# Reordering one layer's late work: raw weights fetched ahead of their casts, r loaded with the decay, bonus halves ahead of y's scaling, the turning copy of an inverse on the engine that makes it

## The chip, the cores and the metric

The kernel runs on one core of a Trainium2 chip. The metric is the device time of one execution in microseconds (us). The core has five engines with an instruction stream each: TensorE (PE, matrix products), VectorE (DVE), ScalarE (ACT), GpSimd (POOL) and SyncE (SP), which here issues every DMA. An engine runs its instructions strictly in the written order.

## The reference

One inference step of a trunk with two layers of width 1024. 1024 prompt tokens (with 16 meta tokens ahead) and 8 sequences of 8 sampled tokens go through it. Layer 0 is a gated DeltaNet, layer 1 an RWKV-7 mixer; a final RMSNorm follows.

```python
def rwkv_mixer(xn, S0, shift_prev, mu, w_rkvz, ...):
    xs = xn[None] + (xprev - xn)[None] * mu[:, None, None, :]         # token shift, mixed per projection
    r, k, v, z = einsum('sbtd,sde->sbte', xs[:4], w_rkvz)             # 1024 x 1024 each
    w = -softplus(-(w0 + tanh(xs[4] @ w1) @ w2)) - 0.5                # decay through a small rank
    a = sigmoid(a0 + (xs[5] @ a1) @ a2)
    kk = l2norm(k * k_k per head);  k = k * (1 + (a - 1) * k_a)
    decay = exp(-exp(w))
    # per head (16 heads of 64), token by token:
    #   S = S * decay - (S kk) (kk a)^T + v k^T ;  y = S r
    # then a GroupNorm per head, + sum(r * k * r_k) * v (the bonus), * silu(z), @ w_o, residual
```

In the kernel the recurrence is done in chunks of 64 tokens; each chunk needs the inverse of a triangular matrix.

## The kernel before, in words

Layer 0 fills the first 1190 us and the norm, the decay and the key projection of layer 1 go on to 1398; the change leaves them alone. What follows has two stages. In both, every engine's order is the order in which the code writes its instructions (a manual schedule); no planner moves anything.

**Projections (1398 to 1782 us).** `projections` writes 67 products of 24 matmuls for r, v and z (tile `d`, a ring of accumulators). After every 12 matmuls comes a gap, and `plan[g]` holds what other engines do in gap `g`, sorted by its last argument: casts and fetches of weight halves (`wraw` raw, `whi` and `wlo` the high and low half of an fp32 number in two narrower ones), the mixes of the token shift, the evacuations `out`. Beside it run the preparations of the recurrence. There are 24 items: 8 head pairs by 3 segments of 384, 384 and 336 tokens. `system_steps` makes each one's decayed keys and stores them (`ald`, `kpd`, `k2d`). Five items make a batch (the last has four). `system_inverse` turns a batch's 120 matrices of 32x32 into inverses (31 steps of two operations, L690 and L692, on GpSimd), ACT copies them transposed (L1647), and SP stores both forms (`r_t`, `r_u`). `system_diagonals` and `system_merge` read them back (`TL`, `sTT`), and `mZ` and `mU` on PE join the 32-blocks to 64-blocks, which go to memory as `ttd`.

**Recurrence (1782 to 2199 us).** `wave` runs 54 steps (`tau`), two per item, so that several items are under way. A step has the phases 0, 1, 1.5, 2 and 3; `put(tau, phase, f, prio)` in `rwkv_item` says where an item's parts are written, and lower `prio` comes first in a phase. Item n starts at T = 2n. Its parts: `load` (cs is the summed decay, r the receptance), `exps` (`fDp`), `reads` (`AR` = r times decay), `pair` (`pr`), `halves` (`prh` on ACT, `prl` on GpSimd), `scores` (`G`), `bonus` (`fbonus` on PE), `keys` (`BT`). `rwkv_finish` scales y with the GroupNorm's factor `grs` on GpSimd (L1953) and multiplies by the gate `lz`. `rTT` is the loaded inverse, `Sb` and `x` are rows of the final norm and the residual sum. `fill`, at prio 2.5 in phase 2 and 1 in phase 3, writes the work that isn't in the chain: what is left of z's product (`dz` and `zo` tiles), and the output projection. Their weights come from `Stream`: `fetch` issues the load of a raw half (L66), `cast` splits it (high on ACT, low on GpSimd), `take` hands one out and refills. Raw halves have two buffers. 58 halves come through it: 10 of z, then 16 for each of the three segments' output projection.

The functions, by line numbers of the profile:

Of the kernel before, what the change touches and what calls it, by code (L numbers as in the profile page):

```python
# [25 lines left out]
class Gaps:  # L26
# [3 lines left out]
    def put(self, g, f, prio=2):  # L30
        self.q.setdefault(max(g, self.now), []).append((prio, f))
# [23 lines left out]
class Stream:  # L55
# [13 lines left out]
    def cast(self):  # L69
        if self.made < len(self.srcs):  # L70
            hi, lo = (self.b.t(self.b.wp, [128, 4, 128], n, self.b.WB, F32R) for n in ("whi", "wlo"))
            self.b.split(self.raw.pop(self.made), hi, lo)
            m = self.srcs[self.made].shape[2]
            self.w[self.made] = [x.rearrange("p a b -> p (a b)").rearrange("p (k m) -> p k m", m=m) for x in (hi, lo)]
            self.made += 1

    def take(self):
        self.used += 1
        while self.made < min(len(self.srcs), self.used + 2):
            self.cast()  # L80
            self.fetch()
        return self.w.pop(self.used - 1)


# [4 lines left out]
class Builder:  # L89
# [581 lines left out]
        L.put(ends[2] + 8, store, 3)  # L671
        return out

    def inverse_open(self, nb, pool):

        T = self.t(pool, [128, 1024], "invT", 1)[0:nb]
        self.nc.gpsimd.memset(T, 0.0)
        self.nc.gpsimd.memset(T[:, 0:1024:33], 1.0)
        return T

    def inverse_steps(self, A, nb, pool, T=None, eng=None):

        nc = self.nc
        v = eng or nc.vector
        T = self.inverse_open(nb, pool) if T is None else T
        Tv = T.rearrange("p (i j) -> p i j", j=32)
        for j in range(31):
            n, m = 31 - j, j + 1
            tmp = self.t(pool, [128, 256], "invtmp", 1)[0:nb, 0:n * m].rearrange("p (n m) -> p n m", m=m)
            v.tensor_tensor(tmp, A[:, j, j + 1:32].unsqueeze(2).broadcast_to([nb, n, m]),  # L690
                            Tv[:, j, 0:m].unsqueeze(1).broadcast_to([nb, n, m]), op=ALU.mult)
            v.tensor_tensor(Tv[:, j + 1:32, 0:m], Tv[:, j + 1:32, 0:m], tmp, op=ALU.subtract)  # L692
            yield Tv
# [880 lines left out]
    def system_steps(self, Q, B):  # L1574

        nc, t, col, pool = self.nc, self.t, self.pcol, B.pool
        pc = lambda x: col[x][:, Q.p:Q.p + 1]
        q = Q.n - B.items[0]
        cs, a, k = (Q.ld[x] for x in ("cs", "a", "k"))
        c6 = lambda x: x.rearrange("p (c i) -> p c i", i=64)  # L1580
        kk, iD = t(pool, [128, 384], "skk", 3), cs
        al, sq = t(pool, [128, 384], "sal", 3), t(pool, [128, 384], "sqs", 3)
        self.act(al[:, 1:384], cs[:, 0:383], AF.Exp, scale=-self.DEC)
        nc.vector.memset(c6(al)[:, :, 0:1], 1.0)
        if Q.s == 0:
            nc.vector.memset(al[:, 0:64].rearrange("p (b r) -> p b r", r=8)[:, :, 0:1], 1.0)
        self.act(sq, k, AF.Square, scale=pc("rwkv_k_k"))
        nc.vector.scalar_tensor_tensor(kk, k, pc("rwkv_k_k"), a, op0=ALU.mult, op1=ALU.mult)
        nc.vector.scalar_tensor_tensor(al, k, pc("rwkv_k_k"), al, op0=ALU.mult, op1=ALU.mult)
        self.act(iD, cs, AF.Exp, scale=self.DEC)  # L1590
        nc.vector.tensor_tensor(kk, kk, iD, op=ALU.mult)
        yield
        self.act(a, a, AF.Identity, scale=pc("rwkv_k_a"), bias=self.omka[:, Q.p:Q.p + 1])
        yield
        ssp = self.ps("f", 2, "rss")
        for c in range(6):
            for h in (0, 1):
                b = slice(64 * h, 64 * h + 64)
                self.mm(ssp[b, c:c + 1], sq[b, 64 * c:64 * c + 64], self.ones[b, 0:1])
        gp = self.ps("f", 2, "L")  # L1600
        for c in range(6):
            for h in (0, 1):
                b, d = slice(64 * h, 64 * h + 64), slice(64 * c, 64 * c + 64)
                self.mm(gp[b, d], al[b, d], kk[b, d])
        nc.vector.tensor_tensor(a, a, k, op=ALU.mult)
        nc.vector.tensor_tensor(a, a, iD, op=ALU.mult)
        nc.sync.dma_start(self.ald[Q.n], al)
        yield
        rk = self.rk2[:, 6 * Q.n:6 * Q.n + 6]
        nc.vector.tensor_scalar(rk, ssp[:, 0:6], 1e-6, None, op0=ALU.add)  # L1610
        nc.vector.reciprocal(rk, rk)
        nc.sync.dma_start(self.kpd[Q.n], kk)
        nc.vector.tensor_tensor(c6(sq), c6(gp[:, 0:384]), rk.unsqueeze(2).broadcast_to([128, 6, 64]), op=ALU.mult)
        if Q.s == 0:
            nc.gpsimd.tensor_tensor(sq[:, 0:64], sq[:, 0:64], self.m_strs2, op=ALU.mult)
        nc.sync.dma_start(self.k2d[Q.n], a)
        yield
        yield
        yield
        nc.sync.dma_start(B.ltd[6 * q:6 * q + 6].rearrange("c q i -> q c i"), c6(sq))  # L1620
# [18 lines left out]
    def system_inverse(self, B):  # L1639

        nc, t, nth, pool = self.nc, self.t, B.nth, B.pool
        nb = 4 * nth
        Av = B.A.rearrange("p (i s) -> p i s", s=32)
        inv = self.inverse_steps(Av.rearrange("p i s -> p s i"), nb, pool, eng=nc.gpsimd)
        for Tv in inv:
            yield
        nc.scalar.copy(Av, Tv.rearrange("p i j -> p j i"))  # L1647
        yield
        ud = self.dram([nb, 1024], f"r{B.b}_u")
        t1d = self.dram([nb // 2, 1024], f"r{B.b}_t")  # L1650
        nc.sync.dma_start(t1d, Tv[0:nb // 2].rearrange("p i j -> p (i j)"))
        nc.sync.dma_start(ud, B.A)
        yield
        yield
        B.TL = t(pool, [128, 30, 32], "TL", 1)[:, 0:nth]
        tv = t1d.rearrange("(c p) (s i) -> p s c i", p=2, s=32)
        for p in (0, 1):
            nc.sync.dma_start(B.TL[64 * p + 32:64 * p + 64], B.ltd[:, 64 * p + 32:64 * p + 64, 0:32].rearrange("c i s -> i c s"))
            nc.sync.dma_start(B.TL[64 * p:64 * p + 32], tv[p])
        B.uv = ud.rearrange("(r c p) (s i) -> r p s c i", r=2, p=2, s=32)  # L1660
# [40 lines left out]
    def rwkv_item(self, n, put):  # L1701

        nc, t, col = self.nc, self.t, self.pcol
        P = Ctx()
        s, p = divmod(n, 8)
# [93 lines left out]
            put(T - 3, 0, lambda: nc.gpsimd.memset(self.UVs[n], 0.0), 4)  # L1799
        if 0 < n < 3:  # L1800
            put(T - 3, 0, lambda: nc.gpsimd.memset(self.TTz[n], 0.0), 4)
        put(*((T - 5, 1) if n else (-4, 0)), lambda: load("cs"), 0)
        put(T - 4, 0, lambda: load("r"), 0.1)
        put(T - 4, 1, lambda: load("k2", "al"), 0)
        put(T - 4, 2, lambda: load("v", "kp"), 0)
        put(*((T - 4, 2) if n else (-3, 1)), exps, 2)
        put(T - 4 if n else -3, 3 if n else 2, reads, 6 if n else -1.5)
        put(T - 1 - (n < 3), 2 + (n < 3), lambda: load("tt"), 0)
        put(T - 3, 2, pair, 1.5)
        put(T - 2, 2, halves, 2.3)  # L1810
        put(T - 2, 1, lambda: scores(0), 2)
        put(T - 2, 2, values, 2.05)
        put(T - 1, 2, bonus, -1)
        put(T - 1, 1, lambda: scores(3), 2)
        put(T - 1, 2, lambda: keys(0), 3)
        put(T - 1, 3, lambda: keys(3), 3)
        if s == 0:
            read = self.rwkv_sample_read(P)
            go = lambda: next(read, None)
# [585 lines left out]
    def projections(self, xa, xb, ip, opened, tiles, whi, wlo, fetch, cast):  # L2405
# [8 lines left out]
        def put(g, f, late=2):  # L2414
            plan[g].append((late, f))
# [63 lines left out]
        for B in batches:  # L2479
            g = g0(B.items[-1]) + 9  # L2480
            B.TT, B.m = {}, {}
            put(g, lambda B=B: self.system_diag(B))
            inv = self.system_inverse(B)
            g = at = max(at + 4, g + 2)
            for u in range(31):
                put(g + u // 2, lambda inv=inv: next(inv, None), 3)
            at += 16
            steps(at, inv, 4, 3)
            g = at + 4
            for q in range(len(B.items)):  # L2490
                put(g + 2 * q + (3 if q == 4 else 0), lambda B=B, q=q: self.system_diagonals(B, q))

                def begin(B=B, q=q):
                    B.m[q] = self.system_merge(B, q)
                    next(B.m[q])
                put(g + 4 + 2 * q, begin)
                for u in range(1, 7):
                    put(g + 4 + 2 * q + u, lambda B=B, q=q: next(B.m[q], None), 1)
# [9 lines left out]
        zin = tuple([f[:, x, k, 0:SEGS[2][1]] for k in range(8)] for x in (0, 1))  # L2508
        self.stream = Stream(self, self.late_weights())
        for u, f_ in ((-1, self.stream.fetch), (-1, self.stream.fetch), (2, self.stream.cast), (2, self.stream.fetch),  # L2510
                      (4, self.stream.cast), (4, self.stream.fetch)):
            put(g + u, f_, 0)

        put(118, opened, 0)
# [8 lines left out]
        for ti, s in order:  # L2523
            m, k = tiles[ti]
            dst = {0: self.rd, 2: self.vd, 3: self.zd}[m]
            for c0, n in SEGS[s:s + 1]:
# [3 lines left out]
                def out(p=p, c0=c0, n=n, m=m, k=k, dst=dst):  # L2530
# [3 lines left out]
                    else:  # L2534
                        nc.scalar.copy(f[:, 0:n], p[:, 0:n])
                    put(now[0] + 2, lambda: nc.sync.dma_start(dst[k][:, c0:c0 + n], f[:, 0:n]))
                put(now[0], out, 0)
        while now[0] < len(plan):
            gap()
        return zin  # L2540
# [1 line left out]
    def wave(self, zin, stay, last, pool):  # L2542
# [63 lines left out]
            put(14 + 16 * s, 3, lambda s=s: residual(s), 4)  # L2606
        for steps, s in more:
            for u, k in steps.items():
                put(*((int(u), 2, lambda s=s, k=k: norm(s, k), 2.55 if s else 2.45) if u == int(u) else (int(u), 3, lambda s=s, k=k: norm(s, k), 5)))

        at = lambda tau: [(P[n], tau - 2 * n) for n in range(max(0, (tau - 4) // 2), min(24, tau // 2 + 1)) if 0 <= tau - 2 * n < 6]
        emit(-4, 3)
# [70 lines left out]
```

## Time and profile before

| what | value |
|---|---|
| three runs | 2209.49, 2211.76, 2212.59 us; median 2211.76 |
| the profiled execution | 2200.45 us; span of its trace 2198.7 us |
| busy share of PE, DVE, ACT, POOL | 95%, 66%, 57%, 57% |
| mean granted clock of PE | 0.981 |
| matmuls | 20958 |
| bytes moved | 291.67 MB, mean 133 GB/s |

The shares are means over the whole span, of which the changed part is the last 800 us. A row of the windows view gives, for a stretch in us, its length and then the busy time of PE, its weight loads, DVE, ACT and POOL with their instruction counts, the clock that PE was granted (1.00 is full), the busy share of the 16 DMA engines, and GB/s. A row of the waits reads: the engine and line that waited, what it waited for, us in total, how often, the longest. A row of the timeline: start, duration, engine, line, operation, tiles, and in brackets the idle time ahead of it and what ended it. A group's row ends with busy us, mean ns of one, idle time before.

### The profile page before, as it was taken

How to read it: one execution, taken by the hardware profiler on the slowest of the kernel's cores; microseconds unless marked ns; L12 is line 12 of the kernel's file. 1: busy time of each engine (PE TensorE's matmuls, PEld its weight loads, DVE VectorE, ACT ScalarE, POOL GpSimd, SP SyncE). 2: the span in 40 equal slices, each digit the busy share in tenths (PEclk: the TensorE clock that was granted, in tenths of full speed). 3: DMA queues.
4: the chain of work that ended last, by engine and by line, in shares of the span. 5: the costliest groups of instructions: out<-in, count | busy, mean ns of one | idle time of the engine just before them, and what ended most of it. 6: DMA issues, size and time to landing. Idle time of an engine off the chain costs nothing.

```text
span 2198.7 us, 56155 instructions
## 1 busy us (share of the span) xinstructions
PE 2084.4 (95%) x20958; PEld 1943.7 (88%) x20958; DVE 1447.7 (66%) x3682; ACT 1261.0 (57%) x3627; POOL 1242.7 (57%) x1858
## 2 busy tenths in 40 slices
PE   8999999999999999989999999998999998899997
PEld 7888989898999989878999999998889986788886
DVE  7868585866757585975436762778656346777865
ACT  6536565656656564645533564755646465676763
POOL 3428677685858585625341451238568645676664
PEclk9999999999999999999999999999999999999998
DMA  4324242424243342426344235587785665665543
GB/s 122 87 71 122 74 126 73 118 72 114 80 118 97 86 124 69 134 72 181 98 136 124 69 107 180 181 253 200 219 250 148 166 181 146 174 170 165 162 129 109
DMA packets 510763, 291.67 MB, mean 133 GB/s; under 512 B 240777, under 2 KB 495866, under 8 KB 510490
## 3 DMA queue, kind: packets, MB, share of 16 engines
q1 hardware_dynamic: 510490, 288.08, 46.7%
q8 instruction: 166, 2.72, 0.5%
q14 instruction: 107, 0.88, 0.1%
HBM read 195.66 MB, written 92.30 MB: 131 GB/s over the span
## 4 chain that ended last, share of the span: by engine, by line
PE 51%; DVE 16%; POOL 9%; issue 8%; DMA 6%; ACT 6%; SPq 3%; DVEq 0%; POOLq 0%; ACTq 0%
PE d L129 13%; PE dz L129 7%; PE dv L129 6%; PE rA L129 5%; PE do L129 3%; DVE cvy L634 3%; POOL y L1953 2%; PE dk L129 2%; PE dq L129 1%; PE dlora L129 1%; PE zo L129 1%; DVE invtmp L690 1%; DVE invT L692 1%; DMA wraw<-in_gdn_w_out 1%; POOL wlo L143 1%
## 5 line engine op out<-in xcount | busy, mean ns | idle before, releaser
L143 POOL TENSOR_TENSOR wlo<-wraw,whi 128x512 fp32r<-128x512 f32 x190 | 255.3, 1344 | 219.7 <-ACT whi L139 204.7
L692 POOL TENSOR_TENSOR invT<-invT,invtmp 72x31 f32<-72x31 f32 (+36 forms) x341 | 213.9, 627 | 26.7
L634 DVE SCALAR_TENSOR_TENSOR cvy<-raw,cw,cvy 128x408 f32<-128x408 f32 (+2 forms) x288 | 203.3, 706 | 29.6 <-ACT cvy L115 25.4
L690 POOL TENSOR_TENSOR invtmp<-invA,invT 72x31 f32<-72x31 f32 (+36 forms) x341 | 203.6, 597 | 26.1 <-DMA invA<-rltd 5.6
L129 PE MATMUL d<-xc,whi 128*128 128x384 f32 (+1 forms) x640 | 177.1, 342 | 0.0
L139 ACT CAST whi<-wraw 128x512 fp32r<-128x512 f32 x238 | 146.0, 615 | 31.3 <-DMA wraw<-in_rwkv_w_o 12.4
L129 PE MATMUL dv<-xc,whi 128*128 128x384 f32 (+1 forms) x480 | 154.2, 342 | 0.0
L129 PE MATMUL dz<-xc,whi 128*128 128x384 f32 (+1 forms) x480 | 152.3, 340 | 0.0
L1953 POOL TENSOR_SCALAR y<-y,mv,grs 128x64 f32<-128x64 f32 x132 | 82.3, 643 | 90.8 <-DVE grs L164 90.8
L115 ACT ACTIVATE w<-rA,nbp 128x128 f32<-128x128 f32 x144 | 45.2, 364 | 153.4 <-PE rA L129 151.0
L129 PEld LDWEIGHTS d<-xc,whi 128*128 128x128 f32 x640 | 118.1, 192 | 2.0 <-ACT ev L1441 0.3
L129 PE MATMUL d<-xc,wlo 128*128 128x384 f32 (+1 forms) x320 | 105.0, 338 | 2.1 <-DVE wlo L143 2.1
L160 POOL TENSOR_TENSOR ors<-ovar,cvals 128x6 f32<-128x6 f32 x24 | 34.1, 1421 | 125.7 <-DVE ovar L1122 125.7
L129 PE MATMUL dz<-xa,whi 128*128 128x384 f32 (+1 forms) x288 | 102.8, 357 | 0.5 <-DVE zg L906 0.5
L129 PE MATMUL d<-xa,whi 128*128 128x384 f32 (+1 forms) x336 | 95.9, 338 | 7.2 <-ACT whi L139 6.0
L129 PE MATMUL dv<-xa,whi 128*128 128x384 f32 (+1 forms) x288 | 102.1, 354 | 0.0
L959 POOL TENSOR_SCALAR Sb<-Sb,eglb 128x128 f32<-128x128 f32 x128 | 88.9, 707 | 5.7 <-DVE usc L752 3.0
L129 PEld LDWEIGHTS dv<-xc,whi 128*128 128x128 f32 x480 | 88.9, 188 | 3.5 <-issue 3.0
L129 PEld LDWEIGHTS dz<-xc,whi 128*128 128x128 f32 x480 | 89.8, 190 | 0.6 <-issue 0.2
L129 PE MATMUL d<-xh,whi 128*128 128x384 f32 (+1 forms) x256 | 82.9, 336 | 0.9 <-ACT xh L139 0.9
L129 PE MATMUL d<-xl,whi 128*128 128x384 f32 (+1 forms) x256 | 83.0, 337 | 0.2 <-DVE xl L143 0.2
L129 PE MATMUL d<-xh,wlo 128*128 128x384 f32 (+1 forms) x256 | 82.5, 336 | 0.0
(557 smaller groups left out, 7288.7 us busy)
## 6 DMA issues: line engine op xcount, KB each, us to landing
wraw<-in_gdn_w_in SPq DMA_DIRECT2D x96, 256.0 KB
wraw<-in_rwkv_w_rkvz SPq DMA_DIRECT2D x74, 256.0 KB
Sb<-in_state_gdn SPq DMA_DIRECT2D x64, 256.0 KB
wraw<-in_rwkv_w_o SPq DMA_DIRECT2D x48, 256.0 KB
E<-drow SPq DMA_DIRECT2D x24, 384.0 KB
attn<-drow SPq DMA_DIRECT2D x24, 384.0 KB
wraw<-in_gdn_w_out SPq DMA_DIRECT2D x36, 256.0 KB
out_s_gdn<-Sb SPq DMA_DIRECT2D x32, 256.0 KB
```

The costliest lines, as they stand in the source:

```text
L115: return self.nc.scalar.activation(out, in_, func, bias=bias, scale=scale, **kw)
L129: self.nc.tensor.matmul(out, lhsT, rhs, start=start, stop=stop)
L139: nc.scalar.copy(hi, x)
L143: e.tensor_tensor(lo, x, hi.bitcast(F32), op=ALU.subtract)
L160: self.nc.gpsimd.tensor_tensor(y, x, half.broadcast_to(sh), op=ALU.pow)
L634: nc.vector.scalar_tensor_tensor(ys[s][:, 0:wd(s)], raws[s][:, k:k + wd(s)], cw[k], ys[s][:, 0:wd(s)], op0=ALU.mult, op1=ALU.add)
L690: v.tensor_tensor(tmp, A[:, j, j + 1:32].unsqueeze(2).broadcast_to([nb, n, m]), Tv[:, j, 0:m].unsqueeze(1).broadcast_to([nb, n, m]), op=AL ...
L692: v.tensor_tensor(Tv[:, j + 1:32, 0:m], Tv[:, j + 1:32, 0:m], tmp, op=ALU.subtract)
L959: nc.gpsimd.tensor_scalar(Sb[g][:, u], Sb[g][:, u], self.eglb[:, hv, 4 * g + u:4 * g + u + 1], None, op0=ALU.mult)
L1953: nc.gpsimd.tensor_scalar(y[:, q], y[:, q], mv[:, q, 0:1], P.rs[:, q:q + 1], op0=ALU.subtract, op1=ALU.mult)
```

## The change

- **Inverses.** The transposing copy moves from ACT to the engine that made the inverse. For batches 0 to 3 this is GpSimd; batch 4's whole inverse (62 operations and the copy) moves to VectorE, three columns per gap from gap 112. The gaps of the batches are now a written table: inverses from 27, 47, 67, 87 and 112, stores and what follows them from 46, 66, 86, 106 and 124. For batches 0 to 3 stores, loads, diagonals and merges are two gaps later than before (44, 64, 84, 104); batch 4's stay (124).
- **Stores and evacuations.** The stores of `ald` and `kpd` are written two gaps and one gap later, each evacuation of `d` one gap later.
- **Stream.** `take` fetches the next raw half and then casts the present one; before, it cast one and fetched the one after the next. One fetch at the start goes. The last 16 low halves are made on VectorE.
- **Loads.** r is loaded together with the decay, three phases earlier.
- **Bonus.** `halves` goes from prio 2.3 to -0.3 in its phase.
- **Others.** `keys(3)` goes ahead of `fill`; the first final norm's parts ahead of it too (2.45 to 0.45).

```diff
@@ Stream @@
-            self.b.split(self.raw.pop(self.made), hi, lo)
+            self.b.split(self.raw.pop(self.made), hi, lo, eng_lo="pool" if self.made < 42 else "dve")
...
         while self.made < min(len(self.srcs), self.used + 2):
+            self.fetch()
             self.cast()
-            self.fetch()
@@ system_steps @@
-        nc.sync.dma_start(self.ald[Q.n], al)
         yield
...
-        nc.sync.dma_start(self.kpd[Q.n], kk)
...
         nc.sync.dma_start(self.k2d[Q.n], a)
         yield
+        nc.sync.dma_start(self.ald[Q.n], al)
+        nc.sync.dma_start(self.kpd[Q.n], kk)
         yield
@@ system_inverse @@
-        inv = self.inverse_steps(Av.rearrange("p i s -> p s i"), nb, pool, eng=nc.gpsimd)
+        eng, tag = (nc.vector, "") if B.b == 4 else (nc.gpsimd, "")
+        inv = self.inverse_steps(Av.rearrange("p i s -> p s i"), nb, pool, eng=eng, tag=tag)
         for Tv in inv:
             yield
-        nc.scalar.copy(Av, Tv.rearrange("p i j -> p j i"))
+        eng.tensor_copy(Av, Tv.rearrange("p i j -> p j i"))
@@ rwkv_item @@
-        put(*((T - 5, 1) if n else (-4, 0)), lambda: load("cs"), 0)
-        put(T - 4, 0, lambda: load("r"), 0.1)
+        put(*((T - 5, 1) if n else (-4, 0)), lambda: load("cs", "r"), 0)
...
-        put(T - 2, 2, halves, 2.3)
+        put(T - 2, 2, halves, -0.3)
...
-        put(T - 1, 3, lambda: keys(3), 3)
+        put(T - 1, 3, lambda: keys(3), 0.5)
@@ projections @@
-            g = at = max(at + 4, g + 2)
+            at, per = (27, 47, 67, 87, 112)[B.b], 3 if B.b == 4 else 2
             for u in range(31):
-                put(g + u // 2, lambda inv=inv: next(inv, None), 3)
-            at += 16
-            steps(at, inv, 4, 3)
-            g = at + 4
+                put(at + u // per, lambda inv=inv: next(inv, None), 3)
+            put(at + 31 // per + 1, lambda inv=inv: next(inv, None), 3)
+            at = (46, 66, 86, 106, 124)[B.b]
+            steps(at, inv, 3, 3)
+            g = at + 3
...
-                      (4, self.stream.cast), (4, self.stream.fetch)):
+                      (4, self.stream.cast)):
...
-                put(now[0], out, 0)
+                put(now[0] + 1, out, 0)
@@ wave @@
-    ... norm(s, k), 2.55 if s else 2.45) ...
+    ... norm(s, k), 2.55 if s else 0.45) ...
```

`inverse_open` and `inverse_steps` take a `tag` that is empty at every call.

The written order at three places. First ACT, in the projections, around the copy that ends batch 0's inverse, before (`mixs` is a mix, `ev` an evacuation, `xa` a mix's high half):

```order
L115 ACTIVATE mixs_19977<-xb_2582_14083,omu_516 128x64
L115 ACTIVATE mixs_19977<-xb_2582_14083,omu_516 128x320
L1647 COPY invA_19275<-invT_19341 120x1024
L2535 COPY ev_20002<-d_19906 128x384
L139 CAST xa_100<-mixs_19972 128x384
```

The same copy after, now on GpSimd (the MEMSETs open batch 1's inverse):

```order
L690 TENSOR_TENSOR invtmp_19947<-invA_19272,invT_19340 120x31
L692 TENSOR_TENSOR invT_19340<-invT_19340,invtmp_19947 120x31
L1648 COPY invA_19272<-invT_19340 120x1024
L677 MEMSET invT_20102 120x1024
L678 MEMSET invT_20102 120x32
L690 TENSOR_TENSOR invtmp_20105<-invA_19869,invT_20102 120x31
```

Nothing on ACT follows the inverse any more. Second GpSimd in the recurrence, the second phase of a step, before (`yl` is the low half of a gated y):

```order
L143 TENSOR_TENSOR yl_27280<-lz_26725,yh_27279 128x384
L143 TENSOR_TENSOR wlo_27295<-wraw_27001,whi_27294 128x512
L160 TENSOR_TENSOR grs_26558<-va_26557,cvals_68 128x6
L1953 TENSOR_SCALAR y_26457<-y_26457,mv_26556,grs_26558 128x64 x6
L1740 COPY DC_27457<-fDp_27455 128x6
L143 TENSOR_TENSOR prl_27466<-pr_27292,prh_27465 128x384
L143 TENSOR_TENSOR wlo_27470<-wraw_27176,whi_27469 128x512
```

And after:

```order
L143 TENSOR_TENSOR yl_27280<-lz_26725,yh_27279 128x384
L143 TENSOR_TENSOR wlo_27297<-wraw_27170,whi_27296 128x512
L160 TENSOR_TENSOR grs_26560<-va_26559,cvals_68 128x6
L143 TENSOR_TENSOR prl_27430<-pr_27292,prh_27429 128x384
L1953 TENSOR_SCALAR y_26455<-y_26455,mv_26558,grs_26560 128x64 x6
L1741 COPY DC_27459<-fDp_27457 128x6
L143 TENSOR_TENSOR wlo_27470<-wraw_27294,whi_27469 128x512
```

`prl` stands ahead of the six scalings of y, behind `grs`'s first step. Third SP in the recurrence's first segment, before (`sso` and `sn` are sample states on their way out and in):

```order
L1727 DMA rTT_4027_23660<-ttd 64x384 x2
L1939 DMA lz_24566<-zd 128x384
L66 DMA wraw_24576<-in_rwkv_w_o 128x4x128
L2028 DMA out_s_rwkv<-sso_24547 64x4x64 x2
L1985 DMA sn_24591<-in_state_rwkv 64x4x64 x4
L1734 DMA fldr_24596<-rd 128x384
L2028 DMA out_s_rwkv<-sso_24547 64x4x64 x2
L1730 DMA BK_24622<-k2d 128x6x64
L1720 DMA AR_24624<-ald 128x6x64
```

And after:

```order
L1735 DMA fldcs_24750<-csd 128x384
L1735 DMA fldr_24752<-rd 128x384
L1728 DMA rTT_4028_23661<-ttd 64x384 x2
L1939 DMA lz_24865<-zd 128x384
L66 DMA wraw_24875<-in_rwkv_w_o 128x4x128
L2028 DMA out_s_rwkv<-sso_24846 64x4x64 x2
L1985 DMA sn_24889<-in_state_rwkv 64x4x64 x4
L2028 DMA out_s_rwkv<-sso_24846 64x4x64 x2
L1731 DMA BK_24918<-k2d 128x6x64
L1721 DMA AR_24920<-ald 128x6x64
```

r's load now stands ahead of the raw fetch (L66) and of the sample states, behind which it stood.

More of the change, by code (lines that the diff above doesn't have):

```diff
@@ L672, in conv_plan, with inverse_open @@
         return out
-    def inverse_open(self, nb, pool):
-        T = self.t(pool, [128, 1024], "invT", 1)[0:nb]
+    def inverse_open(self, nb, pool, tag=""):
+        T = self.t(pool, [128, 1024], "invT" + tag, 1)[0:nb]
         self.nc.gpsimd.memset(T, 0.0)
@@ L679, in inverse_open, with inverse_steps @@
         return T
-    def inverse_steps(self, A, nb, pool, T=None, eng=None):
+    def inverse_steps(self, A, nb, pool, T=None, eng=None, tag=""):
         nc = self.nc
         v = eng or nc.vector
-        T = self.inverse_open(nb, pool) if T is None else T
+        T = self.inverse_open(nb, pool, tag) if T is None else T
         Tv = T.rearrange("p (i j) -> p i j", j=32)
@@ L688, in inverse_steps @@
             n, m = 31 - j, j + 1
-            tmp = self.t(pool, [128, 256], "invtmp", 1)[0:nb, 0:n * m].rearrange("p (n m) -> p n m", m=m)
+            tmp = self.t(pool, [128, 256], "invtmp" + tag, 1)[0:nb, 0:n * m].rearrange("p (n m) -> p n m", m=m)
             v.tensor_tensor(tmp, A[:, j, j + 1:32].unsqueeze(2).broadcast_to([nb, n, m]),
@@ L2608, in wave @@
             for u, k in steps.items():
-                put(*((int(u), 2, lambda s=s, k=k: norm(s, k), 2.55 if s else 2.45) if u == int(u) else (int(u), 3, lambda s=s, k=k: norm(s, k), 5)))
+                put(*((int(u), 2, lambda s=s, k=k: norm(s, k), 2.55 if s else 0.45) if u == int(u) else (int(u), 3, lambda s=s, k=k: norm(s, k), 5)))
         at = lambda tau: [(P[n], tau - 2 * n) for n in range(max(0, (tau - 4) // 2), min(24, tau // 2 + 1)) if 0 <= tau - 2 * n < 6]
```

## The prediction

> **What bounds the kernel now.** I read the page's table of engines first, then windows by stage, then the waits of TensorE (PE) and of the DMA queue, and last the timeline at the stalls.
>
> ```profile
> PE 2084.4 (95%) x20958; PEld 1943.7 (88%) x20958; DVE 1447.7 (66%) x3682; ACT 1261.0 (57%) x3627; POOL 1242.7 (57%) x1858
> core 0: us, PE busy (x) PEld busy (x) DVE busy (x) ACT busy (x) POOL busy (x), PEclk, DMA share, GB/s
> 1398.00:1500.00 102.00, 101.72 (x1042) 98.02 (x1043) 79.02 (x166) 59.75 (x125) 40.47 (x63) 0.97 0.79 240
> 1500.00:1560.00 60.00, 50.75 (x505) 46.98 (x505) 46.28 (x70) 34.02 (x75) 51.51 (x77) 0.89 0.64 174
> 1560.00:1650.00 90.00, 84.66 (x1113) 79.64 (x1112) 51.87 (x102) 48.33 (x102) 49.14 (x84) 0.96 0.88 245
> 1650.00:1782.00 132.00, 126.52 (x1379) 119.91 (x1377) 60.87 (x92) 68.38 (x155) 94.40 (x164) 0.97 0.61 161
> 1782.00:1856.00 74.00, 63.73 (x1130) 54.22 (x1133) 45.31 (x139) 44.59 (x140) 35.33 (x45) 0.93 0.62 159
> 1902.00:2010.00 108.00, 104.78 (x2008) 93.86 (x2008) 83.73 (x258) 78.75 (x260) 74.86 (x94) 1.00 0.60 164
> 2120.00:2199.00 79.00, 61.13 (x680) 55.09 (x673) 44.47 (x142) 34.59 (x108) 38.82 (x43) 0.92 0.37 116
> ```
>
> PE is busy 95% of the span, and the change leaves its matmuls as they are. So a gain can come only from PE's idle time and from time at a lower granted clock. Up to 1398 nothing is touched. In the projections (1398 to 1782) PE idles 0.28 + 9.25 + 5.34 + 5.48 us; in the recurrence the first 74 us lose 10.27. These places the change touches.
>
> **The change part by part.** A minus sign is time saved.
>
> *A. The first inverse and its copy.* Batch 0's inverse is turned by ScalarE (ACT) before; ACT stands until GpSimd (POOL) is done.
>
> ```profile
> 1514.55 2.09 ACT L1647 COPY invA<-invT 120x1024 f32<-120x1024 f32 x1 [9.55 <-POOL invT L692]
> 1524.50 0.69 PE L129 MATMUL d<-xa,whi 128*128 128x384 f32 x1 [5.98 <-ACT whi L139]
> 1518.00:1548.00 30.00, 20.75 (x166) 18.19 (x166) 29.05 (x45) 21.15 (x48) 27.04 (x38) 0.77 0.59 148
> ```
>
> ACT loses 9.55 + 2.09 = 11.64 us, and weights and mixes behind the copy come late. From 1518 to 1548 PE idles 30 − 20.75 = 9.25 us, and at a clock of 0.77 loses 30 × 0.23 = 6.9 us more: 16.2 together. With the copy on GpSimd ACT never stands. What is late next is VectorE (DVE): 29.05 of the 30 us busy. In the other 30 us of the stretch from 1500 to 1560 it is busy 46.28 − 29.05 = 17.23, so most of this is backlog that ACT's stop piled up, not steady load; some of it stays, since its mixes and low halves all come in these gaps. Bounds: nothing, if DVE is the cause, to −16.2. I take −10, nearer to the upper end for that 17.23.
>
> The copy goes onto GpSimd's chain.
>
> ```profile
> L692 POOL TENSOR_TENSOR invT<-invT,invtmp 120x31 f32<-120x31 f32 (+15 forms) x31 | 21.5, 695 | 2.4
> L690 POOL TENSOR_TENSOR invtmp<-invA,invT 120x31 f32<-120x31 f32 (+15 forms) x31 | 20.6, 664 | 2.4
> L677 POOL MEMSET invT<- 120x1024 f32 x1 | 1.0, 957 | 2.6 <-DMA r_t<-invT 2.6
> ```
>
> No row has a copy of this size there: between the memset's 0.96 us and, for a turned copy at a quarter of ACT's pace, 4 × 2.09 = 8.4. The chain of one batch is 21.5 + 20.6 + 2.4 + 2.4 = 46.9 us with its idle time, and with 8.4 it is 55.3, against 20 gaps of about 2.6 us = 52 from one batch's start to the next. Near the memset (I take 2 us) it fits and costs nothing; at 8.4 each later batch slips by 3.3 us, which the third rival takes up. The move of the `ald` and `kpd` stores by two and one gaps, and of the evacuations by one, costs nothing: a store is only read by loads in the recurrence, and four accumulators cover one gap more.
>
> *B. Merges two gaps later, batch 4 on VectorE.*
>
> ```profile
> PE mZ L129 <- DMA sTT<-r_u: 5.2, 2, 2.6
> 1602.70:1605.30 2.60, 0.04 (x2) 0.02 (x1) 1.91 (x4) 1.46 (x4) 2.36 (x4) 1.00 0.83 252
> 1605.50:1608.90 3.40, 3.33 (x31) 3.24 (x31) 3.40 (x4) 2.68 (x8) 3.09 (x5) 0.50 0.59 149
> L690 DVE TENSOR_TENSOR invtmp<-invA,invT 72x31 f32<-72x31 f32 (+15 forms) x62 | 26.9, 433 | 0.6
> L692 DVE TENSOR_TENSOR invT<-invT,invtmp 72x31 f32<-72x31 f32 (+15 forms) x62 | 25.2, 406 | 2.1
> 1713.00:1742.00 29.00, 29.00 (x357) 27.30 (x357) 9.16 (x14) 13.45 (x31) 25.66 (x51) 1.00 0.56 163
> ```
>
> PE waits twice for a merge's load, 5.2 us, and 3.40 us at clock 0.50 follow the first (the second I take alike): 5.2 + 2 × 1.7 = 8.6. Stores and loads move together by two gaps, so the distance between them stays; what changes is which transfers stand in SP's queue around them, at a DMA share of 0.88. Bounds −8.6 to +8.6 (two more such waits); I take −3, as the copy is now done gaps before its store.
>
> Batch 4's 62 operations take (26.9 + 25.2) / 2 = 26.0 us on DVE, in eleven gaps, some 29 us, where DVE has 9.16 of its own: 6.2 us spill into the gaps behind, ahead of the merges (six gaps on). Bounds 0 to +6.2; I take +1.
>
> *C. r loaded with the decay, raw weights fetched ahead of the cast.*
>
> ```profile
> SPq L66 <- POOL wlo L143: 139.6, 39, 8.4
> 1816.98 0.58 SPq L1939 DMA_DIRECT2D lz<-zd  x1
> 1821.02 0.39 SPq L66 DMA_DIRECT2D wraw<-in_rwkv_w_o  x1
> 1826.81 0.60 SPq L1734 DMA_DIRECT2D fldr<-rd  x1
> 1830.72 0.90 DVE L1745 TENSOR_TENSOR AR<-fldr,fDp 128x384 f32<-128x384 f32 x1 [3.78 <-DMA fldr<-rd]
> 1832.14 0.69 PE L129 MATMUL fbonus<-prh,bones 128*128 128x384 f32 x1 [3.56 <-DVE G L1778]
> PE fbonus L129 <- DVE G L1778: 7.6, 3, 3.6
> ```
>
> SP issues in written order. A raw fetch (L66) written behind its cast waits until GpSimd has read the buffer: 139.6 us in 39 waits. Behind it stands r's load, issued 1826.81 and used 3.9 us later; DVE waits 3.78 for it, and the mask of the scores (G) and PE behind. With the fetch written first, its buffer was freed a take earlier; and r is issued with the decay, ahead of the sample state's loads. So DVE's wait of 3.78 goes, and with it most of PE's 7.6. The clock, 0.93 over 74 us, costs 5.2 more. Bounds 0 to −12.8; I take −9, since G then waits for the matmuls of its own scores, which lie close ahead.
>
> *D. Bonus halves ahead of y's scaling.*
>
> ```profile
> 1909.09 4.02 POOL L1953 TENSOR_SCALAR y<-y,mv,grs 128x64 f32<-128x64 f32 x6 [6.27 <-DVE grs L164]
> 1913.21 1.00 POOL L143 TENSOR_TENSOR prl<-pr,prh 128x384 fp32r<-128x384 f32 x1
> PE fbonus L129 <- POOL prl L143: 9.1, 13, 1.9
> ```
>
> GpSimd waits 6.27 us for grs, scales for 4.02, and only then makes prl, which PE wants. Written ahead of the scaling, prl is done at least 4.02 us sooner, more than the longest of the 13 waits (1.9). Cost: one cast earlier on ACT and y 1.0 us later, for which slack is there, as the out-projection takes it a tau later. Bounds 0 to −10.5 (9.1 and some 1.4 of clock); I take −7.
>
> *E. Late state loads, final norm, tail.*
>
> ```profile
> PE rA L133 <- DMA rTT<-ttd: 5.0, 4, 1.6
> PE dyT L129 <- DVE Sb L2088: 2.6, 2, 1.3
> PE fG L129 <- ACT BT L1787: 1.9, 5, 0.4
> ACT whi L139 <- DMA wraw<-in_rwkv_w_o: 12.4, 5, 4.4
> L143 POOL TENSOR_TENSOR wlo<-wraw,whi 128x512 fp32r<-128x512 f32 x190 | 255.3, 1344 | 219.7 <-ACT whi L139 204.7
> L143 DVE TENSOR_TENSOR wlo<-wraw,whi 128x512 fp32r<-128x512 f32 x48 | 40.5, 843 | 33.6 <-ACT whi L139 26.1 <-PE d L129 7.4
> L66 SPq DMA_DIRECT2D wraw<-in_rwkv_w_o x48: 367/390/606, 1821.0 to 2174.7; - x48
> ```
>
> The inverses' loads (rTT) stand behind the same blocked fetch: 5.0 us, bounds 0 to −7.2 with the clock; −4. The first final norm moves ahead of the filling work: 2.6 us, of which −1.5; `keys(3)` moves ahead of it too: at most BT's 1.9 us, taken as nothing, as no wait there is over 0.4. In the tail 16 low halves move: DVE gains 16 × 0.843 = 13.5 us, GpSimd loses 16 × 1.344 = 21.5, in a window where DVE has 44.47 of 79. A low half now stands on DVE ahead of x, which PE waits for; against that it is quicker. Bounds −6 to +8, taken as 0.
>
> **The sum.** −10 − 3 + 1 − 9 − 7 − 4 − 1.5 = −33.5 us. The profiled execution took 2200.45 us (span 2198.7), so 2167.0 on its scale. It lies 11.3 us under the median of the runs, 2211.76, so on their scale the forecast is 2178.
>
> A rule speaks against part of it. The Trainium skill, "TensorE: Matmul & The Clock Gate", section "HAM oscillation — how this bites in real kernels", has the clock drop only after PE gaps over about 3.4 us. By it the gaps in B, D and E would cost no clock; without those parts the sum would be near −30, or 2182. Here a gap of 2.60 us was followed by 0.50 (rows in B), so the trace disagrees; the time by the rule lies inside the range of the forecast and has no chance of its own.
>
> **The rivals.**
>
> *Only the recurrence gains.* DVE's 29.05 of 30 us is a load of its own, and GpSimd's chain ends later by the copy: A and B give nothing or take back 1 to 3. Left are C, D and E, −21.5, +1: 2191. For it: DVE's row and the DMA share of 0.88. Against: DVE's 17.23 in the other 30 us.
>
> *Everything in full.* −16.2 − 8.6 − 12.8 − 10.5 − 7.2 − 2.6 = −57.9, or 2154. Against it: each wait removed leaves the next one close behind.
>
> *Level.* GpSimd's copy costs 8.4 us or more, each batch slips by 3.3 us on the one before, and the fourth's merges come some 13 us late, with PE's clock halved behind each wait: C to E are eaten up to within a few microseconds, 2205 to 2212.
>
> *Slower: raw weights arrive late.* A raw weight is now fetched one take before its cast, where it had two. The 48 fetches lie (2174.7 − 1821.0) / 47 = 7.5 us apart, and a load in this stretch lands 3.9 us after its issue. If takes come in pairs, or SP issues the fetch late, ACT waits: 12.4 / 5 = 2.5 us each in the row in E, in front of PE's chain. With 15 such waits (37 us) the gains are gone; with 20, −33.5 + 50 gives 2228. For it: the five waits of before, with two takes of lead. Against: 7.5 is nearly twice 3.9, and SP is no longer blocked.
>
> That the change doesn't do what it says is excluded for these parts, as the written order shows each move; the new argument `tag` is empty everywhere and does nothing.
>
> **How the numbers follow.** The forecast 0.62, with a range of its own from 2160 to 2188 (A at −16 with C full; A at nothing); only the recurrence 0.18; in full 0.07; level 0.05; slower 0.08. A measurement of this kernel tells about 0.2% (4.4 us) from no change. Faster by more: 0.62 + 0.18 + 0.07 = 0.87; within it 0.05; slower 0.08. The range from 2155 to 2207 leaves out the slower case, most of the level one and some of the full one, under 0.2 together.
>
> **What would show it.** A: no ACT wait before 1524 for invT, PE's idle time from 1500 to 1560 at 3 us or less; wrong, if DVE is again over 29 of 30 us there and PE waits for it. The copy: its row on GpSimd, 2 us or 8. B: mZ waiting for sTT at most once. C: the row of SP's fetch waiting for wlo gone, AR without a wait, at most one G wait over 2 us. D: the prl row under 2 us. E: rTT under 2; ACT's wait for raw weights at 12 or less. More than 15 waits there would make the prediction wrong, as would a new wait of PE on DVE between 1713 and 1782, from batch 4.

## The result and the profile after

Over six runs each the changed kernel took 2169.26 us (median; 2163.34 to 2175.97) against 2207.54 us (2201.12 to 2212.59): the ratio is 0.9831, with a 95% interval of 0.9803 to 0.9859. That is 38 us, where 33.5 were forecast, and lies in the stated range. The profiled execution took 2173.22 us, span 2171.5.

I cut both executions at three marks: the first matmul of the r product, the first bonus product, the last item's bonus product. Of each row the second number is the length. First before, then the changed kernel (windows):

```profile
1398.30:1779.40 381.10, 361.02 (x4010) 342.16 (x4010) 236.24 (x427) 209.13 (x453) 233.23 (x382) 0.96 0.73 204
1779.40:2116.10 336.70, 305.72 (x5688) 269.18 (x5686) 242.79 (x758) 227.76 (x746) 210.93 (x263) 0.97 0.60 163
2116.10:2198.70 82.60, 65.03 (x725) 58.74 (x721) 48.17 (x154) 37.05 (x115) 42.61 (x46) 0.92 0.37 115
```

```profile
1406.70:1783.80 377.10, 358.90 (x4010) 340.34 (x4010) 253.41 (x490) 198.63 (x448) 209.44 (x326) 0.96 0.73 206
1783.80:2085.20 301.40, 290.47 (x5691) 258.60 (x5687) 258.24 (x758) 225.39 (x746) 211.48 (x261) 1.00 0.67 181
2085.20:2171.50 86.30, 67.87 (x725) 61.90 (x721) 54.95 (x170) 36.65 (x115) 23.55 (x30) 0.88 0.36 109
```

The projections fell by 4.0 us, the recurrence by 35.3, and the tail behind its last bonus product grew by 3.7. What lies ahead of 1398, where nothing was changed, took 8.4 us more in this execution. These four make the 27.2 us between the spans, so lengths by stage are compared below, and spans only by medians of many runs. In the recurrence PE's idle time went from 31.0 to 10.9 us and its clock from 0.97 to 1.00; its busy time for the same matmuls fell by 15.3 us.

The waits behind it, in the changed kernel from 1760 us to the end, so with the last 24 us of the projections and the tail (rows of SP, GpSimd and PE):

```profile
SPq L66 <- POOL wlo L143: 13.6, 11, 2.0
POOL prl L143 <- ACT prh L139: 54.9, 22, 6.6
PE rA L133 <- ACT X L115: 5.6, 7, 2.5
PE fVT L126 <- DVE G L1779: 4.3, 2, 3.7
PE fbonus L129 <- DVE G L1779: 0.2, 1, 0.2
```

SP's 139.6 us behind GpSimd's low half are 13.6. PE's rows for prl (9.1) and rTT (5.0) are gone, that for G ahead of the bonus is 0.2. Of the 5.6 us for X, 3.3 lie in the tail; G's 3.7 us (row `fVT`) lie just ahead of the first bonus product. GpSimd now stands 54.9 us for prl's high half ahead of y's scaling, while PE's waits for the y that GpSimd scales are 1.1 us in all. In the projections (two windows, the inverses' groups, a wait):

```profile
1500.00:1560.00 60.00, 57.34 (x554) 54.35 (x553) 52.37 (x84) 35.47 (x78) 54.23 (x75) 0.94 0.77 216
1520.00:1550.00 30.00, 27.34 (x220) 25.58 (x219) 28.57 (x43) 19.11 (x42) 27.07 (x39) 0.89 0.67 180
L1648 POOL COPY invA<-invT 120x1024 f32<-120x1024 f32 x4 | 8.8, 2188 | 0.3
L692 DVE TENSOR_TENSOR invT<-invT,invtmp 96x31 f32<-96x31 f32 (+15 forms) x31 | 10.5, 339 | 1.1
L690 DVE TENSOR_TENSOR invtmp<-invA,invT 96x31 f32<-96x31 f32 (+15 forms) x31 | 10.4, 337 | 0.8
PE mZ L129 <- DMA sTT<-r_u: 8.4, 7, 4.4
```

PE's idle time from 1500 to 1560 is 2.66 us instead of 9.25. VectorE is no less busy there than before: 28.57 of 30 us in the second row, and 29.07 from 1518 to 1548, where it was 29.05. The copy takes GpSimd 2.19 us, batch 4's inverse VectorE 20.9. But the merges' waits rose from 5.2 to 8.4.

### The profile page after: what moved, and what is told of

It is laid out like the page before. It is cut to its first block, busy times and chain, and to the rows that moved or that the text cites. A ratio compares the mean times of both kernels' runs of the same rounds, so it can differ in the third digit from the quotient of the medians.

```text
span 2171.5 us, 56154 instructions
## 1 busy us (share of the span) xinstructions
PE 2072.0 (95%) x20958; PEld 1935.4 (89%) x20958; DVE 1483.7 (68%) x3761; ACT 1247.0 (57%) x3622; POOL 1199.7 (55%) x1784
## 4 chain that ended last, share of the span: by engine, by line
PE 62%; DVE 17%; DMA 7%; ACT 7%; issue 3%; POOL 2%; SPq 2%; DVEq 0%; POOLq 0%; ACTq 0%
PE d L129 13%; PE dv L129 8%; PE dz L129 7%; PE rA L129 6%; PE do L129 3%; DVE cvy L634 2%; PE rA L133 2%; PE dk L129 2%; PE dq L129 2%; PE zo L129 2%; DMA wraw<-in_gdn_w_out 1%; PE xX L133 1%; DVE invtmp L690 1%; DVE invT L692 1%; PE dlora L129 1%
## 5 line engine op out<-in xcount | busy, mean ns | idle before, releaser
L143 POOL TENSOR_TENSOR wlo<-wraw,whi 128x512 fp32r<-128x512 f32 x174 | 231.9, 1333 | 211.8 <-ACT whi L139 181.0
L634 DVE SCALAR_TENSOR_TENSOR cvy<-raw,cw,cvy 128x408 f32<-128x408 f32 (+2 forms) x288 | 201.0, 698 | 31.5 <-ACT cvy L115 27.6
L692 POOL TENSOR_TENSOR invT<-invT,invtmp 72x31 f32<-72x31 f32 (+27 forms) x310 | 196.3, 633 | 24.3
L690 POOL TENSOR_TENSOR invtmp<-invA,invT 72x31 f32<-72x31 f32 (+27 forms) x310 | 186.9, 603 | 21.7 <-DMA invA<-rltd 3.7
L143 DVE TENSOR_TENSOR wlo<-wraw,whi 128x512 fp32r<-128x512 f32 x64 | 49.4, 772 | 50.3 <-ACT whi L139 38.7
L129 PE MATMUL d<-xl,whi 128*128 128x384 f32 (+1 forms) x256 | 82.6, 335 | 0.3 <-DVE sal L1584 0.3
```

The source lines that it names most:

```text
L129: self.nc.tensor.matmul(out, lhsT, rhs, start=start, stop=stop)
L143: e.tensor_tensor(lo, x, hi.bitcast(F32), op=ALU.subtract)
L634: nc.vector.scalar_tensor_tensor(ys[s][:, 0:wd(s)], raws[s][:, k:k + wd(s)], cw[k], ys[s][:, 0:wd(s)], op0=ALU.mult, op1=ALU.add)
```

## The experiments

Ratios are to before, with the 95% interval; medians of the changed kernel and of before from the runs above. The table has each kernel's stages, cut at the same marks, in us. They come from one profiled execution each; where the code of a stage is the same or nearly so they differ by up to 3 us (projections of changed, e2 and e3: 374.1 to 377.1; tails of changed, e2, e3, e4 and e8: 84.8 to 87.2).

| kernel | projections | recurrence | tail |
|---|---|---|---|
| before | 381.1 | 336.7 | 82.6 |
| changed | 377.1 | 301.4 | 86.3 |
| e1_stream_back | 374.2 | 333.9 | 79.2 |
| e2_r_back | 374.1 | 304.1 | 87.2 |
| e3_halves_back | 375.1 | 319.6 | 87.2 |
| e4_copy_on_act | 386.7 | 302.7 | 84.8 |
| e5_rec_only | 384.1 | 300.2 | 84.2 |
| e6_proj_only | 378.1 | 333.4 | 83.5 |
| e7_raw3 | 372.1 | 299.1 | 76.7 |
| e8_merge_later | 379.7 | 300.0 | 85.0 |
| e9_stream_alone | 380.0 | 328.9 | 84.1 |
| e10_halves_alone | 382.1 | 323.7 | 84.1 |
| e11_raw3_lo_gpsimd | 374.8 | 299.2 | 81.9 |
| e12_raw3_batch4_gpsimd | 374.0 | 300.6 | 77.9 |

**e1_stream_back.**

```diff
         while self.made < min(len(self.srcs), self.used + 2):
-            self.fetch()
             self.cast()
+            self.fetch()
...
-                      (4, self.stream.cast)):
+                      (4, self.stream.cast), (4, self.stream.fetch)):
```

> The changed kernel with only the order in the weight stream put back (cast one half, then fetch the one after the next). Theory: SP's fetch again waits behind GpSimd's low half, near 140 us in some 39 waits, and what stands behind it on SP comes late, the inverses' loads (rTT, 5 us on PE before) above all, while r is safe since it is loaded early; the time rises by 7 to 12 us over the changed kernel. Rival (r's early load is all that mattered): 0 to 3 us, and no wait of PE over 1 us in the recurrence that the changed kernel lacks.

2191.65 us, ratio 0.9918 (0.9891 to 0.9944): 22 us by medians over the changed kernel. More than the theory said, and far from the rival. Its waits in the recurrence and its window there:

```profile
SPq L66 <- POOL wlo L143: 111.4, 23, 9.3
PE rA L133 <- DMA rTT<-ttd: 18.9, 14, 4.3
1776.80:2110.70 333.90, 302.38 (x5689) 268.04 (x5687) 259.18 (x757) 225.22 (x746) 212.66 (x263) 0.96 0.60 164
```

With r safe, the blocked SP makes the inverses late: 18.9 us, where before showed 5.0. That r's and prl's lateness stood in front of them there is the likely reason; with prl alone cured (e10) the row stays at 5.8. Idle time is 31.5 us, 20.6 more than in the changed kernel, and PE's busy time 11.9 more at a clock of 0.96. The recurrence is 32.5 us longer, the whole only 22: with the old order a fetch is two takes ahead of its cast again, and the tail is 7.1 us shorter than the changed kernel's.

**e2_r_back.**

```diff
-        put(*((T - 5, 1) if n else (-4, 0)), lambda: load("cs", "r"), 0)
+        put(*((T - 5, 1) if n else (-4, 0)), lambda: load("cs"), 0)
+        put(T - 4, 0, lambda: load("r"), 0.1)
```

> The changed kernel with only r's load put back behind the sample states' loads. Theory: with the fetch no longer blocked, r arrives in time even there; 0 to 3 us over the changed kernel, PE's waits for the masked scores G under 2 us. Rival (r's place is what delayed the scores): G waits of 3 us and more return with halved clock behind them, 8 to 13 us.

2167.84 us, ratio 0.9815 (0.9787 to 0.9843): no difference that shows, as the theory said. r's new place brings no gain that can be measured once the fetch doesn't block.

**e3_halves_back.**

```diff
-        put(T - 2, 2, halves, -0.3)
+        put(T - 2, 2, halves, 2.3)
```

> The changed kernel with only the bonus halves put back behind y's scaling. Theory: PE waits for prl again, about 9 us in 13 waits, with a clock drop or two: 7 to 12 us over the changed kernel. Rival (the waits only showed because the items were late already): 0 to 3 us, prl waits under 3 us in all.

2186.36 us, ratio 0.9891 (0.9862 to 0.9921): 17 us by medians over the changed kernel, above the expectation. PE's row and the recurrence:

```profile
PE fbonus L129 <- POOL prl L143: 14.4, 19, 1.9
1778.40:2098.10 319.70, 297.62 (x5691) 262.50 (x5687) 239.80 (x757) 225.12 (x746) 209.54 (x262) 0.99 0.64 172
```

The waits are 14.4, not before's 9.1, which fits that nothing else is late ahead of them; idle time is 11.2 us more, busy time 7.2.

**e4_copy_on_act.**

```diff
-        eng.tensor_copy(Av, Tv.rearrange("p i j -> p j i"))
+        (eng.tensor_copy if B.b == 4 else nc.scalar.copy)(Av, Tv.rearrange("p i j -> p j i"))
```

> The changed kernel with the transposing copies of batches 0 to 3 back on ScalarE (same gaps; batch 4 stays on VectorE). Theory: ScalarE stands for some 10 us at batch 0's end again, PE waits 6 us for a weight's high half with a halved clock behind it: 4 to 10 us over the changed kernel. Rival (the stall is VectorE's load, not ScalarE's wait, as the projections became only 4 us shorter in the profiles): 0 to 3 us.

2177.72 us, ratio 0.9855 (0.9828 to 0.9883): 8.5 us by medians, 5 by the ratios (whose intervals overlap), 9.6 by the length of the projections. The stall is back (timeline of ScalarE and PE):

```profile
1512.94 2.09 ACT L1648 COPY invA<-invT 120x1024 f32<-120x1024 f32 x1 [8.70 <-POOL invT L692]
1522.88 0.69 PE L129 MATMUL d<-xa,whi 128*128 128x384 f32 x1 [5.12 <-ACT whi L139]
```

The copy's engine is what stood behind this stall. VectorE's load, the rival, is there in both kernels (29.07 of 30 us in the changed one), and without the copy on ScalarE PE waits for it 1.8 us in all between 1500 and 1560.

**e5_rec_only** is before with the hunks of the diff in `Stream` (without the 16 low halves), `rwkv_item`, `wave` and the early fetch; **e6_proj_only** is before with the others of `projections`, `system_steps` and `system_inverse`.

> The kernel before with the recurrence's edits alone: stream order, r's load, bonus halves, keys and first norm's places. Theory: from the first bonus product to the last the time falls by some 35 us, as with the whole change, and the run comes out 32 to 38 us under before, within 5 us of the changed kernel. Rival (the gain needs the projections' edits, which bring the inverses in time): 20 us or less under before, with waits for rTT left.

> The kernel before with the projections' edits alone (copies with the inverse's engine, table of gaps, batch 4 on VectorE, stores and evacuations moved). Theory by the stages of the profiles: 3 to 7 us under before. Rival (my term A and B of before the result): 9 to 14 us under.

e5: 2174.53 us, 0.9850 (0.9819 to 0.9881), 33 us under before. e6: 2202.39 us, 0.9979 (0.9962 to 0.9996), 4.6 us under by the ratio. Both as the theory had it, and together near the 38 of the whole change; the 16 low halves are in neither.

**e7_raw3.** A third raw buffer, from another pool:

```diff
-            w = self.raw[self.fetched] = self.b.t(self.b.wp, [128, 4, 128], "wraw", 2)
+            x = self.fetched % 3 == 2
+            w = self.raw[self.fetched] = self.b.t(self.b.fp if x else self.b.wp, [128, 4, 128], "wraw", 1 if x else 2)
...
-                      (4, self.stream.cast)):
+                      (4, self.stream.cast), (4, self.stream.fetch)):
```

> The changed kernel with a third buffer for raw weights in the stream and the fourth early fetch back, so that a fetch is two takes ahead of its cast and still blocked by none. Theory: ScalarE's waits for raw weights in the recurrence (12.1 us in 7, and 6.6 in 2 at its start) go to under 3 us, but only the ones at the start and in the tail are in PE's way: 2 to 6 us under the changed kernel. Rival (ScalarE had slack there): within 1.5 us of it.

2153.08 us, ratio 0.9763 (0.9735 to 0.9791): 16 us under the changed kernel, far more than expected, and the fastest of all. What the third buffer removes stands in the changed kernel's timeline, first ScalarE at the recurrence's start (behind the second of these casts come z's gate and the first G, for which PE waited 3.7 us in the row `fVT` of the result, with 3.4 us at a clock of 0.50 behind it), then SP, ScalarE and PE in the tail, with the window behind it:

```profile
1771.59 0.62 ACT L139 CAST whi<-wraw 128x512 fp32r<-128x512 f32 x1 [3.30 <-DMA wraw<-in_rwkv_w_rkvz]
1776.20 0.62 ACT L139 CAST whi<-wraw 128x512 fp32r<-128x512 f32 x1 [3.32 <-DMA wraw<-in_rwkv_w_rkvz]
```

```profile
2113.37 4.88 SPq L66 DMA_DIRECT2D wraw<-in_rwkv_w_o  x3
...
2112.31 0.61 ACT L139 CAST whi<-wraw 128x512 fp32r<-128x512 f32 x1
2116.52 0.62 ACT L139 CAST whi<-wraw 128x512 fp32r<-128x512 f32 x1 [3.60 <-DMA wraw<-in_rwkv_w_o]
2117.04 0.51 ACT L115 ACTIVATE X<-xX,rk 128x64 f32<-128x64 f32 x2
...
2117.40 0.37 PE L133 MATMUL rA<-X,rTT 128*64 128x64 f32 x1 [2.48 <-ACT X L115]
2117.00:2123.90 6.90, 6.50 (x44) 6.24 (x45) 4.15 (x13) 2.04 (x8) 0.57 (x1) 0.51 0.13 38
```

Two casts follow one another; the second finds no raw weight and waits 3.60 us, and X behind it on ScalarE, which is in the chain, comes late to PE, which waits 2.48 us and then runs 6.9 us at a clock of 0.51. In e7_raw3, whose lines are numbered one higher (ScalarE's wait; windows of recurrence and tail):

```profile
ACT whi L140 <- DMA wraw<-in_rwkv_w_o: 1.3, 2, 0.9
1774.70:2073.80 299.10, 289.87 (x5690) 258.45 (x5686) 257.81 (x757) 225.03 (x746) 212.01 (x262) 1.00 0.67 184
2073.80:2150.50 76.70, 63.64 (x725) 58.11 (x721) 54.40 (x170) 36.67 (x115) 24.36 (x31) 0.93 0.39 120
```

The tail is 9.6 us shorter than the changed kernel's, the projections with the first steps 5.0, the recurrence 2.3. Only the first is well clear of the scatter: against the projections of e2 and e3, which have nearly the changed kernel's code there, the 5.0 us are 2.0 and 3.0.

**e8_merge_later.**

```diff
-                put(g + 4 + 2 * q, begin)
+                h = g + 4 + 2 * q + (B.b < 4)
+                put(h, begin)
...                                       # its further steps at h + u
```

> The changed kernel with the merges of batches 0 to 3 one gap further behind the loads they need. Theory: PE's waits for the merge's loads (8.4 us in 7, the longest 4.4 with 6.9 us at half the clock behind it) fall under 3 us: 4 to 8 us under the changed kernel. Rival (the transfers are the limit there, at a DMA share of 0.97 to 1.02, and the wait goes to the next reader): 0 to 2 us under.

2171.54 us, ratio 0.9849 (0.9817 to 0.9881): no gain, the projections 379.7 us.

```profile
PE mZ L129 <- DMA sTT<-r_u: 5.0, 2, 4.6
```

The row fell from 8.4 to 5.0, but the long wait stayed at 4.6, and the time didn't fall: the rival. Around the long wait the changed kernel's windows show the DMA engines full for three of four stretches (last but one column):

```profile
1616.00:1620.00 4.00, 4.00 (x48) 3.92 (x45) 2.14 (x7) 1.65 (x4) 3.64 (x5) 1.00 0.97 262
1620.00:1624.00 4.00, 3.56 (x62) 3.08 (x61) 1.75 (x3) 2.22 (x6) 3.58 (x6) 1.00 0.70 229
1624.00:1628.00 4.00, 4.00 (x63) 3.69 (x62) 3.74 (x9) 2.96 (x8) 3.69 (x5) 1.00 1.02 226
1628.00:1632.00 4.00, 1.34 (x29) 0.98 (x27) 1.34 (x2) 0.64 (x2) 3.45 (x8) 1.00 0.96 269
```

That the transfers are the limit there fits this but isn't shown, as no run took any of them away.

**e9_stream_alone** and **e10_halves_alone** are before with the one edit (e1's and e3's diffs, the other way).

> The kernel before with the stream's new order alone (fetch, then cast; one early fetch fewer). Theory: SP's wait behind GpSimd goes, and with it the late r and the late inverses, since undoing it in the changed kernel cost 22 us: 15 to 20 us under before, PE's waits for G and rTT under 2 us each, those for prl grown from 9.1 towards the 14.4 that they had with the halves alone put back. Rival (r's early load is needed too): 8 us or less under before, G waits of 3 us left.

> The kernel before with the bonus halves' place alone. Theory: prl's 9.1 us of waits go, but the items that it no longer holds then wait for the late r and the late inverses, so less is gained than the 17 us that the same edit is worth in the changed kernel: 3 to 9 us under before, rTT and G waits grown by some 3 to 6. Rival (the edits add up): 14 to 18 us under.

e9: 2194.94 us, 0.9946 (0.9927 to 0.9965); e10: 2194.98 us, 0.9945 (0.9925 to 0.9966). Each is worth 12 us, less than theory in the first, between theory and rival in the second. PE's rows, of e9 and then of e10:

```profile
PE fbonus L129 <- POOL prl L143: 12.3, 16, 1.9
PE fbonus L129 <- DVE G L1778: 1.6, 2, 0.8
```

```profile
PE rA L133 <- DMA rTT<-ttd: 5.8, 6, 3.2
PE fbonus L129 <- DVE G L1778: 4.2, 4, 2.7
```

In e9 G and rTT are cured without r's new place, and prl takes over with 12.3. In e10 the wait for rTT stays near before's 5.0 and that for G falls from 7.6 to 4.2; neither grows, as I had expected. By the recurrence's length the two alone give 7.8 + 13.0 = 20.8 us, all edits of this part 36.5 (e5), and taking one back costs 32.5 and 18.2. So the two paths hide each other in part: whichever stays late holds the items. What `keys` and the final norm's place add wasn't run by itself, and some of the 36.5 may be theirs.

**e11_raw3_lo_gpsimd** is e7 without `eng_lo="pool" if self.made < 42 else "dve"`; **e12_raw3_batch4_gpsimd** is e7 with batch 4 on GpSimd, from gap 107, two columns a gap.

> The kernel with the third raw buffer (e7_raw3), and the last 16 low halves back on GpSimd. Theory (the raw weights, not the low halves, held the tail): within 3 us of e7_raw3, its tail of 76.7 us within 3. Rival (VectorE's quicker low halves shorten the tail): 4 to 10 us over e7_raw3.

> The kernel with the third raw buffer (e7_raw3), and batch 4's inverse on GpSimd from gap 107, two columns per gap. Theory (my +1 for VectorE's load was too dear or right): within 2 us of e7_raw3. Rival (VectorE's 26 us there hold up the weights' low halves): 3 to 6 us under it. Third (GpSimd can't finish both in time): 3 us or more over it, with PE waiting for merges after 1740.

e11: 2159.34 us, 0.9790 (0.9769 to 0.9811), 6 us over e7 by medians, with intervals that just overlap, and a tail of 81.9 instead of 76.7: the rival. In its tail PE waits 3.6 us for x, where e7 shows 1.3, and 1.1 for a low half of GpSimd, where e7 shows none. So VectorE's quicker low halves shorten the tail here. e12: 2156.20 us, 0.9778 (0.9753 to 0.9804), 3 us over e7 with overlapping intervals, more than the theory's 2. One wait has grown, from 2.0 us in 2, at batch 4's merges (1769 and 1773), as the third case had it:

```profile
PE mU L130 <- ACT sTT L116: 5.3, 2, 2.7
```

Whether batch 4 on VectorE is worth 3 us or nothing stays open within the noise.

## Why the prediction was right

The direction, the stage and the mechanisms held; the sum did so with errors of both signs. That it came within 5 us of the 38 is partly luck: the projections' edits brought 4.6 us (e6) where A and B had 12, and the recurrence's 33 (e5) where C, D, E and the norm had 21.5.

- **A, the copy: −10 taken, about right.** The stall went as forecast, ScalarE's wait and PE's 5.98 with it. From 1500 to 1560 idle time and lost clock cost 9.25 + 60 × 0.11 = 15.9 us before and 2.66 + 60 × 0.06 = 6.3 after, 9.6 less; e4 gives 8.5 by medians and 9.6 by the stage, though 5 by the ratios. The copy at 2.19 us on GpSimd met the 2 that I took. But my reason was wrong: VectorE's load wasn't backlog (29.07 of 30 us without the stall); it hardly holds PE, which waits for it 1.8 us between 1500 and 1560. And of the two times at half clock that my 6.9 us priced, 1523.6 to 1530.4 and 1540.6 to 1547.5, the second is in the changed kernel too (1540.2 to 1547.0). The stage fell by 4.0 only, as PE waits longer for the merges and 3.7 us ahead of the first bonus product.
- **B: −3 taken, nothing came.** The merges' waits rose to 8.4 us in 7, where I had named one at most. The reason that I gave (the copy done gaps before its store) didn't bear: the loads themselves are late, and e8 shows that one gap more doesn't cure it. The +1 for batch 4 is undecided (e12); its 62 operations took 20.9 us, not 26.0.
- **C, D, E with the norm: −21.5 taken; 33 by e5, 35.3 by the stage.** This is the term mis-sized. Its upper bounds make 33.1: 24.3 us of waits in the rows and 8.8 of clock, of which no row shows the 1.4 in D and the 2.2 in E. I took two thirds, expecting the next wait close behind each one removed. None came: 20.1 us of idle time went, and all of the 17.1 us at half clock, which had cost some 8.5. The other 6.7 us are busy time that neither explains. As the price of one edit the rows were a poor guide, as each path hid part of the others: prl's 9.1 us became 12.3 with the stream cured (e9) and 14.4 with all else cured (e3), rTT's 5.0 became 18.9 (e1). In C the credit went to the wrong part: r's new place gives nothing that shows (e2), and with the fetch ahead of the cast alone G's 7.6 us fall to 1.6 (e9). SP's row for the fetch isn't gone, as I had named, but fell to 13.6.
- **G, the tail** (the last part of E)**: 0 taken, +3.7 by the stage,** of two parts. The late raw weights cost 9.6 us (e7) or 7.1 (e1). The low halves on VectorE save 5.2 where the raw weights come in time (e11 against e7), 3.4 in e1 against before. Where they come late the move saves nothing: without it e5 has a tail of 84.2, the changed kernel 86.3.
- **The slower rival, raw weights arriving late,** had its mechanism right and its number of places wrong: not 15 waits in PE's way but those at the start and in the tail, where takes come in pairs, as it said. ScalarE waited 18.7 us in 9 for raw weights, 12.1 of them for the output projection's, where I had named 12 or less. A third buffer, which cures this, brings 16 us (e7); I had taken nothing for it in the forecast's own sum.
- **The clock.** In the tail a PE wait of 2.48 us was followed by 0.51 for 6.9 us, as the trace of before had it and against the limit of about 3.4 us in the Trainium skill, "TensorE: Matmul & The Clock Gate", "HAM oscillation — how this bites in real kernels". Not every such wait does this: behind one of 2.48 us in e5 (at 2134) and one of 2.56 us in e6 (at 2168) the clock stayed full. What decides wasn't tested.

## What to carry to other kernels

On a queue that issues in written order, a load that waits for its buffer holds every load behind it; look for who suffers behind it, not at the load. Prefetching ahead of the cast with the same two buffers bought freedom from blocking with half the lead; a third buffer gave both, and was worth another 16 us. Where several late inputs meet in one chain, the wait shown for one doesn't price its edit: each of the two edits alone gave 12 us, and taking it back from the whole cost 22 and 17. Taken together the rows were a fair guide, and the lost clock behind them came on top.

## What the runs showed that I had not expected

The first 1398 us, the same code in every kernel here, took from 1398.3 to 1411.8 us in the profiled executions: single spans can't be compared below 13 us, while stages can, down to some 3 us. And the inverse's operations took VectorE 338 ns each on 96 rows here, against 433 and 406 ns on 72 rows in layer 0; why wasn't tried.
